# Places of their own for the values' matmuls in a gated attention and convolution block

## The chip, the core and the metric

The kernel runs on one core of one Trainium2 chip. The time is device time in microseconds (us), the median of several runs. Times inside the program come from one profiled execution.

The engines are named as the profile does: PE is TensorE (PEld its weight loads), DVE is VectorE, ACT is ScalarE, POOL is GpSimd and SP is SyncE, which here only issues DMAs.

## The reference

One layer on 2048 tokens of width 1024, float32. A normalised input is projected into nine parts. Two branches use them: a gated causal convolution of width 3, and attention of 16 query heads on 4 key heads of size 64, each query seeing the last 128 positions and a learned sink. Each branch is multiplied by a SiLU gate, projected, and the two are merged by sigmoid gates, projected once more and added to the input.

```python
h = rms_norm(x, norm_g)
u = jnp.einsum('bsd,dc->bsc', h, w_in)
v_c, b_c, c_c, z_c, q, k, v, z_a, gate_logits = jnp.split(u, SPLIT_POINTS, axis=-1)
y_c = b_c * causal_depthwise_conv(c_c * v_c, conv_w) * jax.nn.silu(z_c)
y_a = jnp.einsum('bsc,cd->bsd', y_c, w_conv_out)
# q and k: rms_norm per head; 128-position blocks, each with the block before it
scores = jnp.einsum('bnqhgd,bnkhd->bnhgqk', qb, kb) * scale
scores = jnp.where(valid[None, :, None, None], scores, NEG_INF)
m = jnp.maximum(jnp.max(scores, axis=-1, keepdims=True), sink)
p = jnp.exp(scores - m)
p = p / (jnp.sum(p, axis=-1, keepdims=True) + jnp.exp(sink - m))
out = jnp.einsum('bnhgqk,bnkhd->bnqhgd', p, vb)
y_b = jnp.einsum('bsc,cd->bsd', o, w_attn_out)       # o: out times its SiLU gate
merged = g_a * y_a + g_b * y_b
return x + jnp.einsum('bsd,de->bse', merged, w_out)
```

## The kernel before

The tokens are worked in two tiles of 1024 (`t` = 0 and 1), each in two halves of 512. A projection of 256 columns is a unit of seven products (a fast scheme of seven in place of eight). [...] The first projection of the first tile has eight plain products; a few units near the start and the end run in pairs.

The order of the work is written out by hand. A counter, `tick`, goes up by one with each product (`run`, L699). Everything else is put on a list under a count (`put`, L693) and is issued right behind the product with that count: in the order in which it was put, three functions first, then the second half of a weight's preparation, then the rest. A "place" in what follows is such a count, relative to the start of the tile. Each engine takes its instructions strictly in this order.

Attention is 32 steps in each tile: four key heads, eight blocks of 128 queries, in that order (`r` = 8 j + b). `attention` (L1657) puts the parts of a step relative to the place `n` of its scores, which stands in `AT0` and `AT1` (L96 to L101):

- n - 5, `att_load`: SP loads queries and keys (L1006 to L1023); n + 4, `att_load_v`: SP loads the values
- n, `att_scores`: six matmuls into the one score tile of PSUM (`ps_s`, one buffer), then on DVE the mask, the maximum and small sums
- n + 1, `att_exp`: four exponentials on ACT (L1079), which read the score tile
- n + 2, `att_norm` and `att_flip`: DVE scales the probabilities and turns 32x32 blocks, and POOL stores them to DRAM (L1099); n + 4, `att_back`: POOL gathers them back turned (L1106)
- n + 9, `att_turn`: ACT casts (L1113, L1114); n + 10, `att_low`: the low part on DVE and four selects on POOL that mask what lies outside the window (L1127)
- n + 13, `att_values`: six matmuls of 256 columns into a bank of `ps_m` (three buffers), L1144
- n + 14, `att_out`: two copies out of PSUM on ACT (L1153); n + 15, `att_sum`: SP stores one half to DRAM, and two places later POOL adds the other half to it (L1160)

The offsets are constants: `V_, F_, B_, X_, L_, O_, S_ = 4, 2, 4, 9, 10, 13, 15` (L57). The step's tiles, among them the four operands of its values, come from a pool of 19 slots in SBUF (`big`), which all results and loads share. A step's functions are put before those of the next step, so where values and a later step's scores have the same place, the values come first.

Of the kernel before, what the change touches and what calls it, by code (L numbers as in the profile page):

```python
# [56 lines left out]
V_, F_, B_, X_, L_, O_, S_ = 4, 2, 4, 9, 10, 13, 15  # L57
# [35 lines left out]
K_WAIT = 10  # L93
H_UP = 3
SUM_WAIT = 6
AT0 = [  # L96
    51, 56, 62, 66, 72, 78, 82, 87, 93, 99, 103, 108, 113, 119, 123, 127, 130, 135, 139, 142, 146, 149,
    153, 156, 160, 164, 167, 170, 174, 177, 181, 184]
AT1 = [
    41, 48, 56, 61, 67, 72, 75, 81, 84, 87, 90, 96, 99, 105, 109, 115, 119, 123, 126, 129, 132, 138,  # L100
    141, 144, 147, 150, 154, 157, 161, 164, 168, 174]  # L101
EVAC = {(0, 0): 3, (1, 1): 4, (0, 1): 5, (1, 0): 6}


# [1 line left out]
def block_kernel(  # L106
# [31 lines left out]
    def slot(shape, dt, name):  # L138
        return big.tile(shape, dt, tag="big", name=name)
# [7 lines left out]
    def mbank(name):  # L147
        return ps_m.tile([P, HB, P], F32, tag="m", name=name)
# [24 lines left out]
    def hs(q):  # L173
        return slice(q * H, (q + 1) * H)
# [178 lines left out]
    def wpair(name):  # L353
        return [wpool.tile([P, KP * UC], F32R, tag="w", name=f"{name}{i}") for i in "hl"]
# [338 lines left out]
    def put(n, f):  # L693
        at.setdefault(max(n, tick[0] + 1), []).append(f)
# [306 lines left out]
    def att_load(t, j, b):  # L1001
        nm = f"{t}_{j}_{b}"
        gb = t * NB + b
        kz = lows[(j * NB + b) % 2]
        q2 = slot([P, 2, 2, P], F32R, f"q2_{nm}")
        nc.sync.dma_start(  # L1006
            q2.bitcast(F32).rearrange("p h c x -> p (h c x)"),
            q2d[t][j][:, 2 * b : 2 * b + 2].rearrange("p h c e x -> p (h c e x)"))

        kq = slot([P, 2, 2 * P], F32R, f"kq_{nm}")  # L1010
        for c in range(2):
            nc.sync.dma_start(
                kq[HALVES[c], 1].bitcast(F32).rearrange("p (h x) -> p h x", h=2),
                q2d[t][j][LH, 2 * b : 2 * b + 2, c].rearrange("p h e x -> p h (e x)"))

        blocks = [(t, b - 1, 0, 2)] if b else [(t, 0, 1, 1)]
        if b == 0 and gb > 0:
            blocks.append((t - 1, NB - 1, 0, 1))
        for kt, k0, to, n in blocks:
            here, there = slice(to * P, (to + n) * P), slice(k0 * P, (k0 + n) * P)  # L1020
            nc.sync.dma_start(kq[:, 0, here].bitcast(F32), kd[kt][j, :, 0, there])
            for c in range(2):
                nc.sync.dma_start(kz[HALVES[c], c, here].bitcast(F32), kd[kt][j, HALVES[c], 1, there])  # L1023
        return q2, kq, kz
# [113 lines left out]
    def att_values(t, j, b, pcv, v2):  # L1138
        xh, xl, y = pcv
        po = mbank(f"po{t}_{j}_{b}").rearrange("p g q -> p (g q)")  # L1140
        for h in range(2):
            cs = slice(h * 2 * P, (h + 1) * 2 * P)
            for n, (kind, xx) in enumerate(((2 + h, xh), (h, y), (2 + h, xl))):
                nc.tensor.matmul(  # L1144
                    po[:, cs], lhsT=v2[:, kind, :], rhs=xx[:, :, h * HD : (h + 1) * HD],
                    start=h == 0 and n == 0, stop=n == 2, skip_group_check=h == 1)
        return po

    def att_out(t, j, b, po):
        pov = po.rearrange("p (h e s c q) -> p h e s c q", h=2, e=2, s=2, c=2)  # L1150
        o = slot([P, 2, 2, P], F32, f"o{t}_{j}_{b}")
        for e in range(2):
            nc.scalar.copy(o[:, :, e].rearrange("p c (h s q) -> p h s c q", h=2, s=2), pov[:, :, e])  # L1153
        return o

    def att_sum(t, j, b, o):
        to = od[t][2 * j : 2 * j + 2, :, b * P : (b + 1) * P].rearrange(
            "c (e d) q -> d (c e) q", d=HD)
        nc.sync.dma_start(to, o[LH].rearrange("p c e q -> p (c e) q"))
        put(tick[0] + ADD_WAIT, lambda: nc.gpsimd.dma_start(  # L1160
            to, o[UH].rearrange("p c e q -> p (c e) q"), accum_op=ALU.add))
# [307 lines left out]
    for t in range(NT):  # L1469
# [9 lines left out]
        for word in (SEQ0, SEQ1)[t].split():  # L1479
            both_ = word.split("+")  # L1480
            for name in both_:
                if len(both_) > 1:
                    paired.add(len(plan))
                key, j = name.rstrip("0123456789"), int(name[-1]) if name[-1].isdigit() else None
                if key in ("ya", "yb"):
                    w = w_co if key == "ya" else w_ao
# [9 lines left out]
    for n in range(S // P // 2):  # L1496
        t, c0 = divmod(2 * n * P, T)
# [7 lines left out]
    def x_state(t):  # L1505
        return state.setdefault(t, {"raw": {}, "ops": {}, "x": {}, "ss": {}})
# [31 lines left out]
    for n in range(KC // 2):  # L1538
        u, h = divmod(n, 2)
        if n < KP - KV_BIG:  # L1540
            live[0] += 2
            w = [[v[:, p * H : (p + 1) * H] for p in range(2)] for v in wpair(f"wkv{n}")]
        else:
            w = [[slot([P, H], F32R, f"wkv{n}_{p}{i}") for p in range(2)] for i in "hl"]
# [109 lines left out]
        ((0, 0), (0, 1), (1, 0), (1, 1), (0, 2), (0, 3), (1, 2), (1, 3)),  # L1654
        ((0, 0), (1, 0), (0, 1), (1, 1), (0, 2), (1, 2), (0, 3), (1, 3)))[KV_ORDER]], kv.banks))

    def attention(t, places):  # L1657
        for r, n in enumerate(places):
            j, b = divmod(r, NB)
            got = {}  # L1660

            def step(k, f, got=got):
                def g():
                    got[k] = f(got)
                return g

            put(n - 5, step("l", lambda g, j=j, b=b: att_load(t, j, b)))
            put(n + V_, step("v", lambda g, j=j, b=b: att_load_v(t, j, b)))
            put(n, step("s", lambda g, j=j, b=b: att_scores(t, j, b, g["l"])))
            put(n + 1, step("e", lambda g, j=j, b=b: att_exp(t, j, b, g["s"])))  # L1670
            put(n + 2, step("n", lambda g: att_norm(g["e"])))
            put(n + F_, step("f", lambda g, j=j, b=b: att_flip(t, j, b, g["n"])))
            put(n + B_, step("b", lambda g, j=j, b=b: att_back(t, j, b, g["f"])))
            put(n + X_, step("x", lambda g, j=j, b=b: att_turn(t, j, b, g["b"])))
            put(n + L_, step("w", lambda g: att_low(g["x"])))
            put(n + O_, step("o", lambda g, j=j, b=b: att_values(t, j, b, g["w"], g["v"])))
            put(n + O_ + 1, step("z", lambda g, j=j, b=b: att_out(t, j, b, g["o"])))
            put(n + S_, step("t", lambda g, j=j, b=b: att_sum(t, j, b, g["z"])))

    def paired_units(units):  # L1680
        (ka, oa, fa), (kb, ob, fb) = units
# [3 lines left out]
    for t in range(NT):  # L1685
        ops = state[t]["ops"]
        ys, opa, opb = {}, {}, {}
        t0 = tick[0] + 1 if t else 1
        a0 = t0 + (14 if t else 0)
        attention(t, [a0 + n for n in (AT0, AT1)[t]])  # L1690

        def unit_of(name, at_of):
            key, j = name.rstrip("0123456789"), int(name[-1]) if name[-1].isdigit() else None
            o = {"ya": opa, "yb": opb}.get(key, ops)
            if key == "k":
                return (key, t), o, fin_k(t)
            if key == "v":
                return (key, t), o, fin_v(t)
            if key == "q":
                fin = fin_q(t, j)  # L1700
            elif key == "cv":
                fin = fin_cv(t, j, ys)
            elif key == "b":
                fin = fin_b(t, j, ys)
            elif key in ("ga", "gb"):
                fin = fin_g(t, int(key == "gb"), j)
            elif key == "z":
                fin = fin_z(t, j, lambda k, q: yd[t][k, :, hs(q)], "z", ("c", t), ycd[t], at_of, nc.sync)
            elif key == "za":
                fin = fin_z(t, j, lambda k, q: od[t][k, :, hs(q)], "za", ("a", t), ocd[t], at_of, nc.gpsimd)  # L1710
            else:
                fin = fin_y(t, int(key == "yb"), j, at_of)
            return (key, t, j), o, fin

        if t + 1 < NT:
            h_stats(t + 1, tick[0] + STATS_AT)
        for word in (SEQ0, SEQ1)[t].split():
            n = tick[0] + 1
            if word == "z0":
                (h_prep if t + 1 < NT else w_prep)(*((t + 1,) if t + 1 < NT else ()), tick[0])  # L1720
            if word == "za2+za3":
                load_set(("c", t), n, opa)
            if word == "ya2+ya3":
                load_set(("a", t), n, opb)
            if word == "yb2+yb3":
                load_set(("h", t + 1) if t + 1 < NT else ("w", 0), n, x_state(t + 1)["ops"])
            names = word.split("+")
            if len(names) > 1:
                paired_units([
                    unit_of(name, lambda e, i=i, n=n: n + 2 * e + i) for i, name in enumerate(names)])  # L1730
            elif t == 0 and word == "q0":
                run(qunit(("q", 0, 0), ops, fin_q(0, 0)))
            else:
                run(sunit(*unit_of(word, lambda e, n=n: n + e)))
# [58 lines left out]
```

## Time and profile before

| | us |
|---|---|
| median of 3 runs | 1880.72 |
| range of the runs | 1880.46 to 1881.01 |
| the profiled execution | 1880.86 |
| its span, first to last instruction | 1878.9 |
| PE busy | 1872.3 |
| DVE busy | 1539.0 |
| ACT busy | 990.7 |
| POOL busy | 728.6 |

Matmuls are pipelined, so the durations of neighbours overlap: how long a group of them holds PE is read from the starts of what comes before and after it, not from a sum of durations. In rows in order of time the first column is the start in us from the span's start, the second the duration in us, and after the operation come the tiles (output<-inputs), the shapes and the count of instructions merged into the row. A bracket at the end is idle time of the engine just before, and what ended it. A row "A <- B: x, n, y" among the waits says that A waited x us for B in n cases, the longest y.

### The profile page before, as it was taken

How to read it: one execution, taken by the hardware profiler on the slowest of the kernel's cores; microseconds unless marked ns; L12 is line 12 of the kernel's file. 1: busy time of each engine (PE TensorE's matmuls, PEld its weight loads, DVE VectorE, ACT ScalarE, POOL GpSimd, SP SyncE). 2: the span in 40 equal slices, each digit the busy share in tenths (PEclk: the TensorE clock that was granted, in tenths of full speed). 3: DMA queues.
4: the chain of work that ended last, by engine and by line, in shares of the span. 5: the costliest groups of instructions: out<-in, count | busy, mean ns of one | idle time of the engine just before them, and what ended most of it. 6: DMA issues, size and time to landing. Idle time of an engine off the chain costs nothing.

```text
span 1878.9 us, 27817 instructions
## 1 busy us (share of the span) xinstructions
PE 1872.3 (100%) x8590; PEld 1560.2 (83%) x8590; DVE 1539.0 (82%) x2540; ACT 990.7 (53%) x2005; POOL 728.6 (39%) x1034
## 2 busy tenths in 40 slices
PE   9999999999999999999999999999999999999999
PEld 7888888888888888888888888888888888888887
DVE  7999888888887889878589988888887779887654
ACT  7665555556765354445456646556566346344321
POOL 2373454457667111021075535655676211121000
PEclk9999999999999999999999999999999999999999
DMA  8785566689989978899367557758888869989653
GB/s 312 181 230 176 146 177 199 179 251 274 275 247 269 319 270 296 281 290 296 101 191 230 179 167 216 206 159 246 254 238 245 279 246 346 320 263 284 221 174 110
DMA packets 270596, 438.96 MB, mean 234 GB/s; under 512 B 42032, under 2 KB 133168, under 8 KB 270448
## 3 DMA queue, kind: packets, MB, share of 16 engines
q1 hardware_dynamic: 211296, 316.23, 51.1%
q0 software_dynamic: 59008, 120.91, 24.8%
q8 instruction: 69, 1.13, 0.2%
q14 instruction: 79, 0.65, 0.1%
q10 hardware_dynamic: 144, 0.03, 0.0%
HBM read 279.48 MB, written 154.42 MB: 231 GB/s over the span
## 4 chain that ended last, share of the span: by engine, by line
PE 96%; DVE 2%; DMA 1%; issue 1%; ACT 0%; SPq 0%; POOL 0%; DVEq 0%; ACTq 0%; POOLq 0%
PE Y L483 33%; PE Vcv L483 5%; PE Xcv L483 5%; PE s L1055 3%; PE po L1144 2%; PE Xgb L483 2%; PE Vgb L483 2%; PE Xz L483 2%; PE Xb L483 2%; PE Vb L483 2%; PE Vga L483 2%; PE Xga L483 2%; PE Vz L483 2%; PE Vo L483 2%; PE Xo L483 2%; PE Xyb L483 2%
## 5 line engine op out<-in xcount | busy, mean ns | idle before, releaser
L1106 POOL DMA_DIRECT2D x<-fd x256 | 143.7, 607 | 80.3 <-DMA fd<-f 37.3
L1127 POOL TENSOR_SCALAR_AFFINE_SELECT xh<-xh 64x512 fp32r<-64x512 f32 x64 | 66.8, 1044 | 127.8 <-DVE xl L265 98.1
L1079 ACT ACTIVATE p<-s,st,rq 128x128 f32<-128x128 f32 x256 | 112.9, 451 | 1.9 <-DMA lows<-kd 1.9
L1099 POOL DMA_DIRECT2D fd<-f x64 | 38.4, 600 | 166.1 <-DVE f L265 158.4
L483 PE MATMUL Xcv<-oph,wcv_ah 128*128 128x512 f32 x256 | 79.0, 390 | 0.0
L1160 POOL DMA_DIRECT2D od<-o x64 | 69.6, 1094 | 19.1 <-ACT zs L1310 7.8
L883 POOL DMA_DIRECT2D q2d<-q_h x56 | 38.8, 692 | 73.8 <-ACT q_h L875 63.1
L1350 POOL DMA_DIRECT2D md<-thyb x32 | 27.4, 873 | 100.7 <-DVE thyb L265 79.0
L1127 POOL TENSOR_SCALAR_AFFINE_SELECT xl<-xl 64x512 fp32r<-64x512 f32 x64 | 63.0, 984 | 4.4
L1127 POOL TENSOR_SCALAR_AFFINE_SELECT yp<-yp 64x512 fp32r<-64x512 f32 x64 | 57.7, 901 | 4.2
L1127 POOL TENSOR_SCALAR_AFFINE_SELECT yp<-xl 64x512 fp32r<-64x512 f32 x64 | 55.8, 872 | 3.1
L483 PEld LDWEIGHTS Xcv<-oph,wcv_ah 128*128 128x128 f32 x256 | 47.6, 188 | 9.5
L265 DVE SCALAR_TENSOR_TENSOR y<-u,cols,y 128x512 f32<-128x512 f32 x64 | 51.5, 805 | 3.7 <-ACT y L1189 2.5
L265 DVE TENSOR_TENSOR opa<-ina,opa 128x512 fp32r<-128x512 f32 x56 | 36.2, 687 | 20.9 <-ACT opa L300 20.9
L265 DVE TENSOR_TENSOR p<-p,st 128x512 f32<-128x512 f32 x64 | 49.3, 770 | 2.7
L1079 ACT ACTIVATION_READ_ACCUMULATOR p<-s,st,rq 128x1 f32 x256 | 51.1, 200 | 0.0
L365 ACT CAST wcv_sh<-wcv_raw 128x1024 fp32r<-128x1024 f32 x16 | 16.9, 1054 | 63.0 <-DVE wcv_raw L265 63.0
L483 PE MATMUL Xcv<-oph,wcv_al 128*128 128x512 f32 x128 | 49.9, 390 | 0.0
L265 DVE STREAM_TRANSPOSE f<-p 128x512 f32<-128x512 f32 x64 | 45.5, 710 | 2.6 <-DVE p L265 0.2
L265 DVE TENSOR_TENSOR opc<-inc,opc 128x512 fp32r<-128x512 f32 x56 | 36.2, 687 | 13.8 <-ACT opc L300 10.3
L483 PE MATMUL Y<-oph,wcv_d 128*128 128x512 f32 x192 | 46.5, 391 | 0.0
L265 DVE TENSOR_REDUCE st<-s 128x4 f32<-128x512 f32 x64 | 44.2, 691 | 2.0
(792 smaller groups left out, 6590.9 us busy)
## 6 DMA issues: line engine op xcount, KB each, us to landing
wcv_raw<-in_w_in SPq DMA_DIRECT2D x32, 512.0 KB, 4.4
q<-q2d SPq DMA_DIRECT2D x64, 256.0 KB, 4.5
v<-vd SPq DMA_DIRECT2D x128, 128.0 KB, 4.3
fd<-f POOLq DMA_DIRECT2D x64, 256.0 KB, 3.9
x<-fd POOLq DMA_DIRECT2D x256, 64.0 KB, 3.3
gd<-th SPq DMA_DIRECT2D x64, 256.0 KB, 3.3
wq_raw<-in_w_in SPq DMA_DIRECT2D x16, 512.0 KB, 5.3
kq<-q2d SPq DMA_DIRECT2D x128, 64.0 KB, 4.4
```

Source lines behind the costliest of these rows:

```text
L265: r = f(*args, **kw)
L365: return (lambda: nc.scalar.copy(hi, src), lambda: vec.tensor_tensor(out=lo, in0=src, in1=hi.bitcast(F32), op=ALU.subtract))
L483: nc.tensor.matmul(ps, lhsT=w[:, j, :], rhs=b[:, m, :], start=start and j == 0 and i == 0, stop=j == KP - 1 and i == 2, skip_group_check=n ...
L883: (nc.sync if t == j == 0 else nc.gpsimd).dma_start(q2d[t][j][half, q * 2 * HB : (q + 1) * 2 * HB, i, e, :], src[HALVES[e]].bitcast(F32).r ...
L1055: nc.tensor.matmul(to, lhsT=w, rhs=x_, start=n == 0, stop=n == 2, skip_group_check=h == 1)
L1079: nc.scalar.activation(out=p[:, i, :], in_=sg[:, i, HD : 3 * HD], func=AF.Exp, bias=st[:, 1, i : i + 1], scale=rv[:, i // 2, i % 2 : i % 2 ...
L1099: nc.gpsimd.dma_start(fd, f)
L1106: nc.gpsimd.dma_start(x[QUADS[k]], src[k])
L1127: nc.gpsimd.affine_select(out=d4, in_=s4, pattern=[[0, 2], [-32 * sg, 2], [0, G], [-sg, 32]], compare_op=ALU.is_gt if prev else ALU.is_ge, ...
L1144: nc.tensor.matmul(po[:, cs], lhsT=v2[:, kind, :], rhs=xx[:, :, h * HD : (h + 1) * HD], start=h == 0 and n == 0, stop=n == 2, skip_group_c ...
L1160: put(tick[0] + ADD_WAIT, lambda: nc.gpsimd.dma_start(to, o[UH].rearrange("p c e q -> p (c e) q"), accum_op=ALU.add))
L1350: nc.gpsimd.dma_start(md[t][k, :, hs(q)], m, accum_op=ALU.add)
```

## The change

The values' matmuls no longer come at a fixed distance behind the scores. Each step has a place of its own for them, in `AV0` and `AV1`; the copies out of PSUM, the store and the accumulating store keep their distances from the values (1, 2 and 4 places). The places of the scores change as well, by up to three, and with them everything that is put relative to them.

```diff
-AT0 = [
-    51, 56, 62, 66, 72, 78, 82, 87, 93, 99, 103, 108, 113, 119, 123, 127, 130, 135, 139, 142, 146, 149,
-    153, 156, 160, 164, 167, 170, 174, 177, 181, 184]
-AT1 = [
-    41, 48, 56, 61, 67, 72, 75, 81, 84, 87, 90, 96, 99, 105, 109, 115, 119, 123, 126, 129, 132, 138,
-    141, 144, 147, 150, 154, 157, 161, 164, 168, 174]
+AT0 = [51, 56, 62, 66, 72, 78, 82, 87, 91, 96, 104, 109, 113, 119, 122, 126, 130, 134, 138, 141, 146, 149, 153, 156, 159, 164, 167, 170, 173, 177, 181, 183]
+AT1 = [41, 48, 56, 61, 67, 72, 75, 81, 85, 88, 91, 97, 100, 106, 110, 116, 120, 124, 126, 129, 133, 138, 141, 144, 147, 150, 154, 157, 160, 163, 167, 173]
+AV0 = [66, 72, 75, 82, 87, 91, 96, 100, 104, 109, 119, 122, 126, 132, 138, 141, 143, 149, 153, 156, 159, 164, 167, 170, 173, 177, 181, 183, 186, 190, 194, 197]
+AV1 = [56, 61, 72, 75, 81, 85, 88, 97, 100, 101, 104, 110, 116, 120, 124, 129, 133, 138, 139, 144, 147, 151, 154, 157, 160, 163, 167, 170, 173, 176, 180, 186]
...
-    def attention(t, places):
-        for r, n in enumerate(places):
+    def attention(t, places, values):
+        for r, (n, o) in enumerate(zip(places, values)):
             j, b = divmod(r, NB)
...
-            put(n + O_, step("o", lambda g, j=j, b=b: att_values(t, j, b, g["w"], g["v"])))
-            put(n + O_ + 1, step("z", lambda g, j=j, b=b: att_out(t, j, b, g["o"])))
-            put(n + S_, step("t", lambda g, j=j, b=b: att_sum(t, j, b, g["z"])))
+            put(o, step("o", lambda g, j=j, b=b: att_values(t, j, b, g["w"], g["v"])))
+            put(o + 1, step("z", lambda g, j=j, b=b: att_out(t, j, b, g["o"])))
+            put(o + S_ - O_, step("t", lambda g, j=j, b=b: att_sum(t, j, b, g["z"])))
...
-        attention(t, [a0 + n for n in (AT0, AT1)[t]])
+        attention(t, *([a0 + n for n in at_] for at_ in ((AT0, AV0), (AT1, AV1))[t]))
```

## The prediction

> **What bounds the kernel now.** I read the page's busy times, clock and chain first, then TensorE's waits, then its instructions in order of time around the attention's matmuls.
>
> ```profile
> span 1878.9 us, 27817 instructions
> PE 1872.3 (100%) x8590; PEld 1560.2 (83%) x8590; DVE 1539.0 (82%) x2540; ACT 990.7 (53%) x2005; POOL 728.6 (39%) x1034
> PEclk9999999999999999999999999999999999999999
> PE 96%; DVE 2%; DMA 1%; issue 1%; ACT 0%; SPq 0%; POOL 0%; DVEq 0%; ACTq 0%; POOLq 0%
> ```
>
> TensorE is busy throughout, at full clock in every slice, and 96% of the chain that ended last is its own.
>
> ```profile
> PE Y L1525 <- DVE zero L182: 1.5, 1, 1.5
> PE Vq L483 <- DVE wq_sl L265: 0.5, 1, 0.5
> ...
> PE Y L483 <- DVE yap L265: 0.2, 1, 0.2
> ```
>
> These are the first, second and last rows of what TensorE waited for: no score and no value matmul stands there. So the program lasts as long as the row of matmuls does, and a change counts in two ways: it alters how long that row takes with nothing to wait for, or it puts a wait into it. The number of matmuls, their shapes and their work stay as they are.
>
> The unit of time is one product of twelve matmuls, which is one place in the lists that the change edits:
>
> ```profile
> 602.88 0.61 PE L483 MATMUL Xz<-oph,wz_ah 128*128 128x512 f32 x2
> ...
> 605.60 0.61 PE L483 MATMUL Vz<-oph,wz_sh 128*128 128x512 f32 x2
> ...
> 608.32 0.61 PE L483 MATMUL Y<-oph,wz_sh 128*128 128x512 f32 x2
> ```
>
> Starts of undisturbed products lie 2.72 us apart.
>
> **What a neighbour is worth.** The six score matmuls (L1055) of a step and its six value matmuls (L1144) are put between products. I price a group from its own start to the start of the second product behind it, less one undisturbed product. That takes in whatever the group does to the product that follows it.
>
> ```profile
> 232.06 0.33 PE L1055 MATMUL s<-lows,kq 128*128 128x384 f32 x1
> ...
> 232.85 2.92 PE L483 MATMUL Y<-oph,wb_d 128*128 128x512 f32 x12
> 235.62 0.28 PE L1144 MATMUL po<-xh,v 128*128 128x256 f32 x1
> ...
> 236.33 0.63 PE L483 MATMUL Xcv<-oph,wcv_ah 128*128 128x512 f32 x2
> ...
> 239.08 0.61 PE L483 MATMUL Vcv<-oph,wcv_sh 128*128 128x512 f32 x2
> ...
> 1082.77 0.28 PE L1144 MATMUL po<-xh,v 128*128 128x256 f32 x1
> ...
> 1083.49 0.34 PE L1055 MATMUL s<-lows,kq 128*128 128x384 f32 x1
> ...
> 1084.28 2.91 PE L483 MATMUL Y<-oph,wcv_d 128*128 128x512 f32 x12
> 1087.03 0.61 PE L483 MATMUL Xb<-oph,wb_ah 128*128 128x512 f32 x2
> ...
> 1433.25 0.28 PE L1144 MATMUL po<-xh,v 128*128 128x256 f32 x1
> ...
> 1437.50 0.62 PE L483 MATMUL Vz<-oph,wz_sh 128*128 128x512 f32 x2
> ```
>
> Scores alone: 235.62 - 232.06 - 2.72 = 0.84 us. Values alone: 239.08 - 235.62 - 2.72 = 0.74 us. Values directly in front of scores, which the kernel before has seven times: 1087.03 - 1082.77 - 2.72 = 1.54 us, and in the last of them 1437.50 - 1433.25 - 2.72 = 1.53 us. Worked in nanoseconds from the same rows, every merged group costs 1533, every one of 37 undisturbed groups of values 739 or 740, and 40 of 44 of scores 833 (the other four are the narrow first blocks, at 700). So a merge saves 833 + 740 - 1533 = 40 ns. Where it comes from can be seen: inside the merged group nothing is saved, but the product behind scores takes 235.62 - 232.85 = 2.77 us and the one behind a merged group 1087.03 - 1084.28 = 2.75 us, so two slowed products become one.
>
> [...]
>
> **The change, part by part.** The lists in the diff, with the old rule that values come 13 places behind their scores, give the count of merges: 1 of 32 steps in the first tile and 6 in the second before, 24 and 24 after (values whose place stands in the scores' list of the tile). That is 48 - 7 = 41 more, so 41 x 0.040 = 1.64 us less. Both ends for the two merges with narrow scores, which no row shows: 0 and 0.07 us each, the slow-down behind both groups being some 0.04 and 0.03; I take 0.04.
>
> Scores move by at most three places, values by up to four, and with them every instruction that hangs on them: a step's loads on SP's queue, its exponentials and casts on ACT, its mask and four gathers on POOL, its store and accumulating store. Their number doesn't change. ACT (53%) and POOL (39%) have room in total; what matters is what arrives late somewhere, and there are three such things.
>
> First, scores. All scores share one PSUM tile, so a step's scores wait until the previous step's exponentials have read theirs. Before, neighbours were at least three places apart. After, two pairs are two apart: 181 and 183 in the first tile, 124 and 126 in the second. From the end of a score group (0.36 us after its last matmul's start) to the start of the next lies 2 x 2.72 + 0.83 - 0.96 = 5.31 us in the second tile, where 0.96 is 1084.09 + 0.36 - 1083.49 by the rows here and above. In the first tile values stand in front of the second scores, which gives 5.31 + 0.74 = 6.05 us. How long the exponentials take:
>
> ```profile
> 1084.09 0.36 PE L1055 MATMUL s<-lows,kq 128*128 128x384 f32 x1
> 1320.27 0.36 PE L1055 MATMUL s<-lows,kq 128*128 128x384 f32 x1
> 1100.63 0.33 PE L1055 MATMUL s<-lows,kq 128*128 128x384 f32 x1
> ...
> 1101.22 0.36 PE L1055 MATMUL s<-lows,kq 128*128 128x384 f32 x1
> 550.97 0.36 PE L1055 MATMUL s<-lows,kq 128*128 128x384 f32 x1
> 1200.11 0.36 PE L1055 MATMUL s<-lows,kq 128*128 128x384 f32 x1
> ```
>
> ```profile
> 1089.66 0.46 ACT L1079 ACTIVATE p<-s,st,rq 128x128 f32<-128x128 f32 x1
> 1325.83 0.45 ACT L1079 ACTIVATE p<-s,st,rq 128x128 f32<-128x128 f32 x1
> 1109.32 0.45 ACT L1079 ACTIVATE p<-s,st,rq 128x128 f32<-128x128 f32 x1
> 551.79 0.65 ACT L1153 COPY o<-po 128x256 f32<-128x256 f32 x2
> 554.87 0.21 ACT L1076 ACTIVATE st<-st 128x4 f32<-128x4 f32 x1 [2.42 <-DVE st L265]
> 556.28 0.46 ACT L1079 ACTIVATE p<-s,st,rq 128x128 f32<-128x128 f32 x1
> 558.48 0.62 ACT L1113 CAST xh<-x 128x512 fp32r<-128x512 f32 x1
> 1203.85 0.45 ACT L1079 ACTIVATE p<-s,st,rq 128x128 f32<-128x128 f32 x1
> ```
>
> The end of the last exponential less the end of the scores is 8.19 us at its longest (1109.77 - 1101.58) and 3.83 at its shortest (1204.30 - 1200.47). It goes with the place inside a projection's seven products, since ACT and DVE prepare weights there: place 124 is the sixth of seven, and the four scores that stood sixth in the second tile before took 4.85 to 5.96 us, the first 5.67 (1090.12 - 1084.45), the last 5.66, their mean 5.54. So scores at 126 would wait 5.54 - 5.31 = 0.23 us, with the ends at 0 and 8.19 - 5.31 = 2.88. For the first tile the step at 181 stays where it is, with 5.41 us (556.74 - 551.33) against 6.05: no wait. The copies of the output (0.65 us) already stand ahead of its exponentials, and the casts of another step (0.62 us and as much again) that now come ahead too fit into the 2.42 us that ACT waits there for DVE. Without that cover 5.41 + 1.24 - 6.05 = 0.60 us. Behind a waiting score stand the next product and all that follows.
>
> Second, values wait for POOL's masks. The tightest cases before:
>
> ```profile
> 501.30 0.76 POOL L1127 TENSOR_SCALAR_AFFINE_SELECT xl<-xl 64x512 fp32r<-64x512 f32 x1
> 1153.31 0.76 POOL L1127 TENSOR_SCALAR_AFFINE_SELECT xl<-xl 64x512 fp32r<-64x512 f32 x1
> ```
>
> ```profile
> 502.58 0.28 PE L1144 MATMUL po<-xh,v 128*128 128x256 f32 x1
> 1155.97 0.28 PE L1144 MATMUL po<-xh,v 128*128 128x256 f32 x1
> ```
>
> The masks end 0.52 us ahead at the first, which the change gives a place more. Of the 64 steps 29 get one to three places more and 35 keep 13; the tightest of those 35 has 1155.97 - 1154.07 = 1.90 us. POOL would have to be that much later there before TensorE notices. I take 0.
>
> Third, holding. A step's four operands of the values live up to three places longer, and their SBUF slots are free later for loads and results. No wait of TensorE goes back to that now. I take 0, with one product (2.72 us) as the other end.
>
> Sum: -1.64 + 0.23 = -1.41 us. The profiled execution took 1880.86 us (span 1878.9 and 1.96 around it), 0.14 over the median of 1880.72; so 1879.45 for it and **1879.3 us** as a median, 0.07% less. A measurement of this kernel tells about 0.2% (3.76 us) from no change, so this counts as the same.
>
> **The rivals.** (a) The merges are given back by one wait: scores two places apart. It decides at the second tile's pair, once the exponentials end later than 5.31 + 1.64 = 6.95 us after the scores; from there on the kernel is slower than before. For it: the output's copies stand ahead of most exponentials now, and the longest row is 8.19. Against it: the sixth place of that tile was never over 5.96. At 8.19 the time is 1880.72 - 1.64 + 2.88 = 1882.0.
>
> (b) A merge saves nothing, because the slowed product belongs to any dense stretch and doubles with its length. Against it: seven merged groups at 1533 ns. Time: 1880.72 + 0.23 = 1881.0. [...]
>
> (c) Masks come late. Two score pairs closer together crowd POOL. If it were 3 us later everywhere, the margins of the 35 unmoved values would be short by 5.7 us in all: 1879.3 + 5.7 = 1885.0. Against it: for any wait at all it takes 1.9 us.
>
> (d) Loads or products wait for held slots, one product's length: 1879.3 + 2.7 = 1882.0.
>
> (e) The matmuls don't come to stand together, because something of TensorE's lies between values and scores in one place. The only others are turnings: of keys and values early in a tile, of the norms after the first tile's last scores. Time: 1880.7 plus 0.2.
>
> **How the numbers follow.** The forecast 0.64 (from 1878.9, with no wait, to 1880.2), (a) 0.13, (b) 0.06, (c) 0.08, (d) 0.06, (e) 0.03. The likeliest is 1879.3. The low end, 1878.6, is the full 1.64 with the narrow merges at their upper end and the 0.3 us by which single runs lie below the median; the high end, 1882.2, takes in (a), (b), (d) and (e) and leaves out most of (c) and the worst of (a). Faster by over 0.2% would need 3.76 us, and no row offers more than 41 x 0.07 = 2.9: 0.04. Slower by over 0.2% is (c) in most of its size and two bad waits of (a) or (d): 0.09. Within: 0.87.
>
> **What would show it.** Right: 48 merged groups at 1533 ns, 16 alone of each kind, no score or value among TensorE's waits except scores near the 126th place of the second tile with some tenths; a span of about 1877.5. Wrong: a wait of over 1.6 us there (a); merged groups at 1573 ns (b); values waiting for masks in POOL's rows (c); products waiting for weights prepared late on ACT or DVE, which I priced at nothing.

## The result, and the profile after

| us | before | after |
|---|---|---|
| median | 1880.87 (4 runs, 1880.46 to 1881.40) | 1906.21 (4 runs, 1904.59 to 1909.31) |
| the profiled execution | 1880.86 | 1909.31 |
| its span | 1878.9 | 1906.8 |
| groups of values directly in front of scores | 7 | 48 |
| idle stretches of PE over 0.1 us, in all | 3.0 | 20.1 |
| half clock granted | none | 13.65 |

The ratio is 1.0135 (95% interval 1.0124 to 1.0147): the kernel became 25.3 us slower, where 1.4 us less was forecast. Lines above the lists have their old numbers in the changed kernel, those behind stand two earlier (PE's products are L481, scores L1053, values L1142).

The page of the kernel after: its span, the busy times and the chain that ended last.

```profile
span 1906.8 us, 27817 instructions
PE 1883.0 (99%) x8590; PEld 1564.2 (82%) x8590; DVE 1538.6 (81%) x2540; ACT 989.6 (52%) x2005; POOL 735.6 (39%) x1034
PE 85%; DVE 5%; DMA 4%; issue 2%; ACT 2%; POOL 1%; SPq 0%; ACTq 0%; DVEq 0%; POOLq 0%
```

The counts of instructions are the same and so is the work of DVE and ACT. PE's own share of the chain fell from 96% to 85%; DVE, DMA and ACT have taken it. What PE waited for, kernel after:

```profile
PE Y L481 <- DVE b L263: 4.2, 1, 4.2
PE Y L481 <- ACT Y L504: 3.2, 2, 2.2
PE po L1142 <- POOL yp L1125: 2.5, 2, 2.2
PE s L1053 <- ACT p L1077: 2.3, 1, 2.3
PE po L1142 <- POOL xl L1125: 1.7, 2, 1.3
```

Before, the longest was the 1.5 us at the start. Now four single waits are over 2 us (the row of ACT's Y holds one of them, of 2.2), and only one of them is a score's. The span grew by 27.9 us: 17.1 is idle time of PE, 6.8 is an estimate for the 13.65 us at half clock (half of it is lost, as the product of 4.60 us below shows), and 1.6 goes off for the merges; that leaves 5.6 us, which lies in PE's busy time and which I haven't assigned.

Whether the change did what it says is seen in PE in order of time, a merged group of the kernel after:

```profile
259.27 0.28 PE L1142 MATMUL po<-xh,v 128*128 128x256 f32 x1
259.99 0.34 PE L1053 MATMUL s<-lows,kq 128*128 128x384 f32 x1
...
263.53 0.62 PE L481 MATMUL Y<-oph,wcv_sh 128*128 128x512 f32 x2
```

It costs 263.53 - 259.27 - 2.72 = 1.54 us, as the seven groups of before did.

**The half clock.** PE in order of time, kernel after, and the same time in slices of a microsecond (busy time and count of each engine, granted clock, DMA share, GB/s):

```profile
1339.23 0.36 PE L1053 MATMUL s<-lows,kq 128*128 128x384 f32 x1
1343.78 4.60 PE L481 MATMUL Y<-oph,wb_d 128*128 128x512 f32 x12 [4.19 <-DVE b L263]
```

```profile
1344.00:1345.00 1.00, 1.00 (x4) 0.77 (x4) 1.00 (x2) 0.00 (x0) 1.00 (x3) 0.59 0.55 166
1345.00:1346.00 1.00, 1.00 (x4) 0.80 (x3) 0.93 (x3) 0.00 (x0) 1.00 (x2) 0.50 0.75 177
...
1347.00:1348.00 1.00, 1.00 (x5) 0.78 (x4) 1.00 (x3) 1.00 (x2) 0.00 (x0) 0.70 0.84 200
```

The product behind the wait takes 4.60 us, where one behind scores took 2.92 in the prediction's rows. Its slices have a clock of 0.50 for 2 x (0.41 + 0.30) + 2 = 3.42 us, and 4.60 - 2.92 = 1.68 us come on top of the wait. In this profile each of the four waits over 2 us (2.22, 2.17, 2.30 and 4.19) has such a stretch behind it, and no shorter wait has one; other runs below don't keep to that, as the last section shows. The page's row of the clock is the same before and after, since its slices are 48 us long.

**Where the waits come from.** Three are followed back here, each in the kernel after; the fourth, which ends at 414 us, stands at the place that the experiments on order look at. First, values that wait for their masks (DVE, POOL and PE in order of time):

```profile
483.25 0.72 DVE L263 STREAM_TRANSPOSE f<-p 128x512 f32<-128x512 f32 x1 [5.89 <-DMA od<-o]
...
484.27 0.60 POOL L1097 DMA_DIRECT2D fd<-f  x1 [5.14 <-DVE f L263]
487.06 1.69 POOL L1125 TENSOR_SCALAR_AFFINE_SELECT yp<-xl 64x512 fp32r<-64x512 f32 x1
...
488.80 0.38 PE L1142 MATMUL po<-yp,v 128*128 128x256 f32 x1 [2.17 <-POOL yp L1125]
```

`f` is written by DVE from `p`; it has nothing to do with the store of an output `o`, except that it gets a slot of `big`. The release by that store says that the slot was `o`'s and that its accumulating store was not done. DVE stands 5.89 us with all that is queued behind it, POOL, which has the masks behind `f`'s store, stands 5.14 us, and in the end the values wait.

Second, the wait of 4.19 us above: DVE's `b` got the slot of a result `y` whose store was under way. DVE:

```profile
1337.71 0.71 DVE L263 STREAM_TRANSPOSE f<-p 128x512 f32<-128x512 f32 x1 [4.02 <-issue]
...
1343.03 0.69 DVE L263 TENSOR_TENSOR b<-Y,s5b 128x512 f32<-128x512 f32 x1 [2.83 <-DMA yd<-y]
```

`b` reads the PSUM tile Y, and the next product writes it. The slot accounts for 2.83 of the 4.19 us; without it `b` would still have been some 1.4 us late, behind a DVE that had stood 4.02 us just before, for a reason that the profile doesn't name.

Third, the scores at 183 in the first tile (PE, then ACT and DVE in order of time):

```profile
562.53 0.36 PE L1053 MATMUL s<-lows,kq 128*128 128x384 f32 x1
571.36 0.45 PE L1053 MATMUL s<-lows,kq 128*128 128x384 f32 x1 [2.30 <-ACT p L1077]
...
565.73 0.69 ACT L1217 ACTIVATE th<-Xga,hbias 128x512 f32<-128x512 f32 x1 [4.30 <-PE Y L481]
566.32 0.61 ACT L363 CAST wz_d<-wz_raw 128x512 fp32r<-128x512 f32 x1
...
566.96 0.69 DVE L263 TENSOR_TENSOR wz_d<-wz_raw,wz_d 128x512 fp32r<-128x512 f32 x1 [4.06 <-ACT wz_d L363]
569.34 0.21 ACT L1074 ACTIVATE st<-st 128x4 f32<-128x4 f32 x1 [0.70 <-DVE st L263]
...
570.76 0.46 ACT L1077 ACTIVATE p<-s,st,rq 128x128 f32<-128x128 f32 x1
```

The exponentials of the step at 181 end 8.33 us behind its scores (571.22 - 562.89), not 5.41 as before. Their sums on DVE stand behind a weight's `wz_d`, and that behind the same weight's cast on ACT, which stands behind the tanh of a result. In the kernel before the tanh began 0.3 us after its product had given way to the next group of matmuls (550.70 and 550.38); here it begins 4.5 us after that (565.73 and 561.22), released by the next product. Whether it waited for a slot there, the trace doesn't say.

**Stores that hold slots.** A view that the prediction didn't use is the idle time of DVE and ACT that ends with a store of `o`, `y` or `f`. The instructions released read none of these stores' data; they write tiles that get slots of `big`, so by the inferred releaser this is time lost to slots. The kernel before, all five rows:

```profile
DVE b L265 <- DMA fd<-f: 2.0, 1, 2.0
ACT th L1219 <- DMA fd<-f: 2.6, 1, 2.6
ACT xh L1113 <- DMA od<-o: 2.5, 1, 2.5
ACT yp L1114 <- DMA od<-o: 2.3, 2, 1.8
ACT o L1153 <- DMA od<-o: 0.6, 1, 0.6
```

The kernel after, its four largest:

```profile
DVE f L263 <- DMA od<-o: 5.9, 1, 5.9
DVE b L263 <- DMA yd<-y: 2.8, 1, 2.8
...
ACT p L1077 <- DMA od<-o: 5.8, 3, 3.4
ACT p L1077 <- DMA fd<-f: 4.7, 1, 4.7
```

The sum is 10.0 us before and 26.4 after; I call it "slot waits" below. The count isn't complete: idle time of ACT and DVE in front of tiles of `big` for which the profile names no releaser ("issue") is left out, 23.9 us before and 26.8 after. Before, no slot wait was over 2.6 us, and apart from the 1.5 us at the start TensorE waited 0.5 us at most for anything. The pool had little slack already.

### The profile page after: what moved, and what is told of

Its sections match the earlier page's. It is cut to its first block, busy times and chain, and to the rows that moved or that the text cites. A ratio compares the mean times of both kernels' runs of the same rounds, so it can differ in the third digit from the quotient of the medians.

```text
span 1906.8 us, 27817 instructions
## 1 busy us (share of the span) xinstructions
PE 1883.0 (99%) x8590; PEld 1564.2 (82%) x8590; DVE 1538.6 (81%) x2540; ACT 989.6 (52%) x2005; POOL 735.6 (39%) x1034
## 4 chain that ended last, share of the span: by engine, by line
PE 85%; DVE 5%; DMA 4%; issue 2%; ACT 2%; POOL 1%; SPq 0%; ACTq 0%; DVEq 0%; POOLq 0%
PE Y L481 29%; PE Vcv L481 4%; PE Xcv L481 4%; PE s L1053 2%; PE Xz L481 2%; PE Vz L481 2%; PE Xza L481 2%; PE Vo L481 2%; PE Xo L481 2%; PE Vza L481 2%; PE Xga L481 2%; PE po L1142 2%; PE Xb L481 2%; PE kv L570 2%; PE Xgb L481 2%
## 5 line engine op out<-in xcount | busy, mean ns | idle before, releaser
L1097 POOL DMA_DIRECT2D fd<-f x64 | 42.9, 671 | 137.4 <-DVE f L263 134.2
L481 PE MATMUL Xcv<-oph,wcv_ah 128*128 128x512 f32 x256 | 78.9, 390 | 0.0
L1125 POOL TENSOR_SCALAR_AFFINE_SELECT yp<-xl 64x512 fp32r<-64x512 f32 x64 | 62.0, 968 | 3.1
L481 PEld LDWEIGHTS Xcv<-oph,wcv_ah 128*128 128x128 f32 x256 | 47.9, 188 | 9.5
L263 DVE TENSOR_TENSOR xl<-x,xh 128x512 fp32r<-128x512 f32 x64 | 43.6, 681 | 7.7 <-ACT wga_th L363 2.2
L481 PE MATMUL Xcv<-oph,wcv_al 128*128 128x512 f32 x128 | 49.8, 389 | 0.0
L1053 PE MATMUL s<-lows,kq 128*128 128x384 f32 (+2 forms) x128 | 44.3, 346 | 2.7 <-ACT p L1077 2.3
```

What stands on the lines that cost most here:

```text
L263: r = f(*args, **kw)
L481: nc.tensor.matmul(ps, lhsT=w[:, j, :], rhs=b[:, m, :], start=start and j == 0 and i == 0, stop=j == KP - 1 and i == 2, skip_group_check=n ...
L1053: nc.tensor.matmul(to, lhsT=w, rhs=x_, start=n == 0, stop=n == 2, skip_group_check=h == 1)
L1097: nc.gpsimd.dma_start(fd, f)
L1125: nc.gpsimd.affine_select(out=d4, in_=s4, pattern=[[0, 2], [-32 * sg, 2], [0, G], [-sg, 32]], compare_op=ALU.is_gt if prev else ALU.is_ge, ...
```

## The experiments

In the expectations, H is the theory that slots of `big` are held too long, P that the scores' new places do the harm by themselves, and C that the output's copies in front of the exponentials do. The order of the work on ACT, DVE and POOL in general is what is left if all three fall short; the later expectations call it Q. Medians in us; the kernel before ran again beside each group of kernels, at 1880.7 to 1881.1. "Over" is the difference from it; slot waits, merged groups, PE's idle time and the time at half clock (without a stretch that begins in the last 2 us of the span) are of the profiled execution. Single runs of one changed kernel lie up to 6.7 us apart (place_135, 1892.9 to 1899.6), so a few us between two of them decide nothing.

| kernel | median | ratio (95%) | over | slot waits | merged | PE idle | half clock |
|---|---|---|---|---|---|---|---|
| after | 1906.21 | 1.0135 (1.0124 to 1.0147) | 25.3 | 26.4 | 48 | 20.1 | 13.65 |
| scores_only | 1895.05 | 1.0078 (1.0055 to 1.0101) | 13.9 | 15.6 | 20 | 11.2 | 3.4 |
| values_only | 1896.64 | 1.0081 (1.0052 to 1.0111) | 15.5 | 25.8 | 53 | 14.4 | 3.4 |
| hold_15 | 1907.17 | 1.0137 (1.0108 to 1.0167) | 26.1 | 53.4 | 17 | 20.1 | 17.1 |
| copies_behind | 1904.83 | 1.0125 (1.0095 to 1.0155) | 23.7 | 26.6 | 48 | 19.2 | 10.2 |
| after_20 | 1895.08 | 1.0077 (1.0047 to 1.0106) | 14.4 | 24.8 | 48 | 12.8 | 6.8 |
| hold_20 | 1890.82 | 1.0052 (1.0029 to 1.0075) | 10.1 | 13.7 | 17 | 11.1 | 0 |
| before_20 | 1884.26 | 1.0020 (1.0009 to 1.0032) | 3.5 | 7.6 | 7 | 5.4 | 0 |
| before_18 | 1902.55 | 1.0116 (1.0087 to 1.0146) | 21.8 | 41.5 | 7 | 17.0 | 6.8 |
| late_casts | 1912.42 | 1.0168 (1.0138 to 1.0197) | 31.4 | 28.1 | 48 | 23.0 | 10.2 |
| values_late | 1910.34 | 1.0157 (1.0127 to 1.0186) | 29.3 | 31.1 | 53 | 23.7 | 17.1 |
| values_14 | 1890.59 | 1.0053 (1.0034 to 1.0073) | 9.6 | 24.1 | 26 | 9.2 | 0 |
| scores_20 | 1884.76 | 1.0022 (1.0010 to 1.0035) | 3.7 | 5.8 | 20 | 6.8 | 3.4 |
| after_v8 | 1900.35 | 1.0099 (1.0071 to 1.0128) | 19.6 | 20.2 | 48 | 14.7 | 0 |
| hold_v8 | 1890.72 | 1.0046 (1.0023 to 1.0069) | 9.9 | 16.4 | 17 | 10.2 | 0 |
| before_v8 | 1883.36 | 1.0015 (1.0003 to 1.0026) | 2.6 | 4.6 | 7 | 5.8 | 3.4 |
| after_20_v8 | 1897.38 | 1.0087 (1.0061 to 1.0113) | 16.6 | 5.8 | 48 | 14.9 | 6.8 |
| place_135 | 1896.13 | 1.0077 (1.0043 to 1.0110) | 15.1 | 26.5 | 48 | 14.9 | 10.2 |
| values_20 | 1899.82 | 1.0095 (1.0072 to 1.0118) | 18.8 | 20.7 | 53 | 17.2 | 6.8 |

### The parts of the change alone

scores_only has the new places of the scores, and values 13 behind them as in the kernel before (here and below some lists are written as the rule that gives them):

```diff
+AV0 = [n + 13 for n in AT0]
+AV1 = [n + 13 for n in AT1]
```

> The places of the scores are those of the change, and the values come 13 places behind their scores again, as in the kernel before: 20 merges in place of 48 (7 before), no step is held longer. Theory P (the new places of the scores are to blame: scores stand where ACT and DVE are busy with weights, and two pairs are only two places apart): most of the loss stays, 15 to 25 us over before. Theory H (operands held longer, so that slots of the pool come free late): within 3 us of before. Theory C (the output's copies in front of the exponentials on ACT): a third of the loss, 4 to 8 us over before.

values_only keeps the scores' old places and moves values alone, 13 to 16 behind, so that 53 groups are merged:

```diff
+AV0 = [66, 72, 78, 82, 87, 93, 95, 103, 108, 113, 119, 123, 127, 135, 139, 142, 146, 149, 153, 156,
+       160, 164, 167, 170, 174, 177, 181, 184, 187, 190, 194, 197]
+AV1 = [56, 61, 72, 75, 81, 87, 90, 96, 99, 100, 105, 109, 115, 119, 123, 129, 132, 138, 141, 144,
+       147, 154, 157, 158, 161, 164, 168, 170, 174, 177, 181, 187]
```

> The scores keep the places of the kernel before; the values go to the first place of a later step's scores that is 13 to 16 places behind their own scores: 53 merges, and 90 step-places of longer holding in sum against 52 in the change. Theory P: the merges bring what they promised, 46 x 0.04 = 1.8 us under before, to 1879. Theory H: worse than the change, 25 to 40 us over before. Theory C: 20 to 30 us over before, as there are as many merges as in the change.

hold_15 keeps the scores' places too and has all values 15 behind, so that what is late is not what is merged:

```diff
+AV0 = [n + 15 for n in AT0]
+AV1 = [n + 15 for n in AT1]
```

> The scores keep the places of the kernel before; every step's values come 15 places behind them in place of 13: 17 merges in place of 7, and 128 step-places of longer holding in sum against 52 in the change. Theory P: 10 x 0.04 = 0.4 us under before. Theory H: 30 us or more over before. Theory C: 3 to 6 us over before.

copies_behind is the change with the two copies out of PSUM put behind the exponentials of the same place:

```diff
-            put(o + 1, step("z", lambda g, j=j, b=b: att_out(t, j, b, g["o"])))
+            copies.append((o + 1, step("z", lambda g, j=j, b=b: att_out(t, j, b, g["o"]))))
...
+        for n, f in copies:
+            put(n, f)
```

> The change as it is, but the copies of the values out of PSUM are issued behind all other attention functions of their place, so behind the exponentials that they stood in front of on ACT. Theory C: the loss goes, within 4 us of before. Theories P and H: the loss stays, 20 to 30 us over before.

Measured: 13.9 and 15.5 us over for the two halves of the change, each a loss by itself; no theory had a range that holds either. hold_15, with 17 merged groups and every score where it was, loses as much as the whole change (26.1, where H had 30 or more), so merging is not what costs. Order of time on ACT and then PE, hold_15:

```profile
594.71 0.62 ACT L1112 CAST yp<-x 64x512 fp32r<-64x512 f32 x1 [6.21 <-DMA od<-o]
597.30 0.59 ACT L504 COPY Y<-Xz 128x512 f32<-128x512 f32 x1
...
597.94 0.80 PE L481 MATMUL Y<-oph,wz_sh 128*128 128x512 f32 x2 [3.18 <-ACT Y L504]
```

A cast gets a slot of an `o` that is still being stored, ACT stands 6.21 us, and the copy into Y, queued behind, lets PE wait 3.18 us. copies_behind gives 1.6 us back, with intervals that overlap: theory C falls as the main cause.

### One slot more, one fewer

For a twentieth slot one of the two spare tiles that hold a sum (`s5`) is given up, and a unit that runs beside another takes a slot in its place. The same is done to the unchanged kernel, which shows the price of the edit itself.

```diff
-    big = ctx.enter_context(tc.tile_pool(name="big", bufs=19))
+    big = ctx.enter_context(tc.tile_pool(name="big", bufs=20))
...
-    def spare(name):
-        return consts.tile([P, H], F32, tag="s5", bufs=2, name=name)
+    def spare(name, other=False):
+        if other:
+            return slot([P, H], F32, name)
+        return consts.tile([P, H], F32, tag="s5", bufs=1, name=name)
...
-        s5 = spare(f"s5{nm}")
+        s5 = spare(f"s5{nm}", other)
```

> The change with 20 slots in the shared pool in place of 19 (the room comes from the second buffer of the spare tile of a projection, which only paired units need; there it takes a slot). Theory H (the pool runs out: an instruction gets the slot of a result whose store is not done, and its engine's whole queue waits): half of the loss or more goes, under 1893. Theory P (places of the scores): the loss stays, 1900 to 1910.

> The kernel with scores as before and values 15 places behind, with 20 slots. Theory H: from 1907 to under 1890, and the waits of ACT for the accumulating store go. Theory P has no word on it, since the scores are where they were; a third theory Q (the later values fall among other work in the queues, whatever the slots) says that it stays within 5 us of 1907.

> Control: the kernel before with 20 slots. Theory H: 0 to 4 us faster than before, as it hardly waits for a slot; P and Q: the same, within 2 us.

before_18 changes the unchanged kernel in one number:

```diff
-    big = ctx.enter_context(tc.tile_pool(name="big", bufs=19))
+    big = ctx.enter_context(tc.tile_pool(name="big", bufs=18))
```

> The kernel before with 18 slots in place of 19, nothing else changed. Theory H: slower by 10 us or more, with waits of ACT and DVE for stores. Theories P and Q: within 3 us of before.

Measured: one slot fewer costs the kernel before 21.8 us, with every place as it was. Among its waits, of DVE, ACT and PE:

```profile
DVE f L265 <- DMA od<-o: 3.7, 1, 3.7
ACT th L1219 <- DMA fd<-f: 6.3, 1, 6.3
...
PE Y L483 <- DVE yap L265: 7.8, 2, 5.2
```

So a pool that is one slot short makes such waits by itself. One slot more takes 16.0 us from hold_15 (26.1 to 10.1, 6.6 above before_20) and 10.9 from the change. So holding is a cause. It isn't all: after_20 stays 10.9 us above before_20, and after_20 and hold_20 (1895.1 and 1890.8) stay just above H's bounds of 1893 and 1890. H also had before_20 at 0 to 4 us faster; it is 3.5 slower, so the edit has a price of its own.

### Holding less in other ways

late_casts is the change, and values_late is values_only, with the loads of the values, the casts and the masks put relative to the values and not to the scores, so that operands are held no longer than before (the gathered probabilities, one tile, are held longer in their place):

```diff
-            put(n + V_, step("v", lambda g, j=j, b=b: att_load_v(t, j, b)))
+            put(o - O_ + V_, step("v", lambda g, j=j, b=b: att_load_v(t, j, b)))
...
-            put(n + X_, step("x", lambda g, j=j, b=b: att_turn(t, j, b, g["b"])))
-            put(n + L_, step("w", lambda g: att_low(g["x"])))
+            put(o - O_ + X_, step("x", lambda g, j=j, b=b: att_turn(t, j, b, g["b"])))
+            put(o - O_ + L_, step("w", lambda g: att_low(g["x"])))
```

> The change with 19 slots, but a step's load of values, its casts and its masks keep their distances to its values (9, 4 and 3 places ahead) in place of those to its scores. A step that waits longer then holds one tile longer (the gathered probabilities), where the change holds four (the values and three operands). Theory H (slots): a good part of the loss goes, from 1906 to 1885 to 1896. Theory P (places of the scores): what the scores' places cost by themselves, 14 us, stays, 1893 to 1897. Theory Q (work falls elsewhere in the queues): 1900 or more.

> Scores where they were before, values merged as in the run that moved values only (53 merges), and load, casts and masks move with the values, so that one tile is held longer in place of four; 19 slots. Theory H: from 1896.6 to 1879 to 1887. Theory Q: 1893 or more.

values_14 keeps the scores' old places and moves values by one place at most, where that merges:

```diff
+AV0 = [n + 14 if n + 14 in AT0 else n + 13 for n in AT0]
+AV1 = [n + 14 if n + 14 in AT1 else n + 13 for n in AT1]
```

> Scores where they were before; values go to a later step's scores only where these are 13 or 14 places behind their own: 26 merges (7 before), 19 step-places of longer holding in sum against 90 in the run that moved values only; 19 slots. Theory H: a fifth of that run's 15.5 us, so 2 to 5 us over before, less 0.8 for the merges. Theory Q: 1888 or more.

scores_20 is scores_only with the slot more:

```diff
-    big = ctx.enter_context(tc.tile_pool(name="big", bufs=19))
+    big = ctx.enter_context(tc.tile_pool(name="big", bufs=20))
...
+        s5 = spare(f"s5{nm}", other)
```

> Only the scores moved, values 13 places behind them, 20 slots. Theory H: from 1895 to 1884 to 1888, as far as 20 slots take it in the kernel before (1884). Theory P: it stays at 1893 to 1897.

Measured: the two with late casts are the slowest of all (31.4 and 29.3). What PE waits for in late_casts:

```profile
PE po L1142 <- POOL yp L1125: 6.3, 4, 2.2
PE po L1142 <- POOL xl L1125: 5.3, 6, 1.5
```

Ten waits of values for masks, 11.6 us: the casts, up to three places later now, come to stand with other work, and the masks stand three places ahead of their values, where the change had up to six. Slot waits didn't fall either (28.1 and 31.1). So these two don't measure the holding. values_14 loses 9.6 us with 26 merged groups, more than the 2 to 5 that H had: either a single place of holding is felt, or the order of the work is. scores_20 stands 0.2 us above before_20, as H had it, so the scores' new places by themselves cost nothing that can be seen once there is a slot more: theory P falls.

### The loads of the values four places later

This shortens the holding of one operand and moves only an issue on SP's queue:

```diff
-V_, F_, B_, X_, L_, O_, S_ = 4, 2, 4, 9, 10, 13, 15
+V_, F_, B_, X_, L_, O_, S_ = 8, 2, 4, 9, 10, 13, 15
```

> The change with 19 slots, but each step loads its values 8 places behind its scores in place of 4, still 5 places (13.6 us) or more ahead of the values' matmuls. Only SP's queue changes; every step holds a slot 4 places shorter, 256 slot-places in sum, against 208 that the change holds more (52 places, four tiles). Theory H (slots run out): half of the loss or more goes, from 1906 to under 1893. Theory Q (the order of work in the queues of ACT, DVE and POOL, whatever the slots): within 4 us of 1906.

> Scores as before, values 15 places behind, loads of the values 8 behind, 19 slots. Theory H: from 1907 to under 1893; theory Q: within 4 us of 1907.

> Control: the kernel before with loads of the values 8 places behind the scores. Theory H: as with 20 slots, within 4 us of before on either side; Q: the same.

> The change with 20 slots and the values loaded 8 places behind the scores. Theory H: 1879 to 1887, so that nothing is left that slots do not explain. Theory Q: what 20 slots left, 10 us or more over before.

Measured: 16.2 us off hold_15, about what the slot gave (16.0), and 5.7 off the change, between H (under 1893) and Q (within 4 us of 1906). With both, the change's slot waits are down to 5.8 us, less than the 10.0 of the kernel before, and it still stands 16.6 us over. The longest slot wait of that run is 1.8 us, and idle time without a named releaser in front of tiles of `big` is 25.0 us there, against 23.9 before. PE's largest waits in after_20_v8 (the edit for the slot moves the lines behind it down by two):

```profile
PE Y L481 <- ACT Y L506: 4.2, 4, 2.6
PE Vcv L481 <- DVE y L263: 1.9, 1, 1.9
PE Y L481 <- DVE b L263: 1.7, 1, 1.7
```

H alone falls as the whole explanation. Nor do the repairs add: after_20 with 24.8 us of slot waits is no slower than after_20_v8 with 5.8.

### Order, at one place

In after_20 the largest wait of PE for ACT stands at 414 us. There the step whose scores are at 134 (135 before) has its exponentials in front of ACT's copy into Y. place_135 puts this one step back:

```diff
-AT0 = [51, 56, 62, 66, 72, 78, 82, 87, 91, 96, 104, 109, 113, 119, 122, 126, 130, 134, 138, 141, 146, 149, 153, 156, 159, 164, 167, 170, 173, 177, 181, 183]
+AT0 = [51, 56, 62, 66, 72, 78, 82, 87, 91, 96, 104, 109, 113, 119, 122, 126, 130, 135, 138, 141, 146, 149, 153, 156, 159, 164, 167, 170, 173, 177, 181, 183]
```

> The change with 20 slots and one number altered: the scores of step 17 of the first tile at place 135, where the kernel before had them, in place of 134. At 134 their exponentials are issued one product earlier, in front of ACT's copy into Y that the next projection's third product needs; in the profile with 20 slots that copy came at 413.6 us and TensorE lost 1.8 us there and more behind it. Theory Q (order): that wait goes, and 2 to 4 us with it, from 1895 to 1891 to 1893. Theory H (slots) has no word on a single place: the wait of TensorE at 412 us stays.

values_20 is values_only with the slot more (its diff is that of after_20):

> Scores where they were before, values merged as in the run that moved values only (53 merges, 1896.6 with 19 slots), with 20 slots. Theory H: 1881 to 1885, no more than the kernel before with 20 slots (1884.3) less the 1.8 us of the merges. Theory Q: over 1888.

ACT and PE in order of time, after_20, and then ACT in place_135:

```profile
413.20 0.46 ACT L1079 ACTIVATE p<-s,st,rq 128x128 f32<-128x128 f32 x1
413.64 0.60 ACT L506 COPY Y<-Xgb 128x512 f32<-128x512 f32 x1
...
414.29 0.73 PE L481 MATMUL Y<-oph,wgb_sh 128*128 128x512 f32 x2 [2.45 <-ACT Y L506]
```

```profile
410.68 0.58 ACT L506 COPY Y<-Xgb 128x512 f32<-128x512 f32 x1
411.39 0.44 ACT L1079 ACTIVATE p<-s,st,rq 128x128 f32<-128x128 f32 x1
```

The copy is some 3 us earlier and the wait is gone, so order at this place is shown as its cause. But the median is about the same, 1896.1 against 1895.1: other waits grew (one of DVE's `b` for a slot lets PE wait 4.3 us in that run, 3.7 in after_20). Q had 1891 to 1893 for it: two of the four runs lie at 1893 and two at 1899, the profiled one among the latter, so what the place is worth in time stays open. values_20 is not helped by the slot either: 18.8 us over, against 15.5 without it. Its largest wait, DVE and PE:

```profile
1303.50 0.71 DVE L263 STREAM_TRANSPOSE f<-p 128x512 f32<-128x512 f32 x1 [6.06 <-DMA od<-o]
...
1311.08 4.20 PE L481 MATMUL Y<-oph,wgb_d 128*128 128x512 f32 x9 [5.74 <-DVE th L263]
```

Still a slot: and over before_20 the loss is 15.3. One slot more doesn't make up for 49 of 64 steps whose operands are held one to three places longer. No version beats the kernel before.

## Why the prediction was wrong

- **The saving of a merge**: right. There are 48 merged groups, 40 of them at 1533 ns; of the 16 scores alone 13 cost 833, and of the 16 values alone 12 cost 739 or 740, as priced. So about 41 x 0.040 = 1.64 us is in the result. values_only shows that it can't be seen beside the rest: 53 merged and 15.5 us slower. Rivals (b) and (e) fall.
- **First, scores**: the second tile's pair loses 0.13 us, where I had 0.23. The first tile's pair waits 2.30, where I had none. The casts did fit into the cover that I named: behind them ACT still waits 0.70 us for DVE. What failed is that the 5.41 us of the old row were carried over to a place whose neighbours on ACT and DVE had moved. This is rival (a) in the other tile, and 2.3 of 25.3 us plus its half clock.
- **Second, masks**: waits of 4.2 us in all stand there, at values whose masks had been in time. The one that was followed back is 2.17 us of a DVE that stood for a slot 5.89 us earlier, not the crowding on POOL that rival (c) assumed.
- **"Third, holding"** is the step that failed: "I take 0, with one product (2.72 us) as the other end". The reason that I gave, that no wait of TensorE goes back to it, looked at one engine only. The runs show in its place a cost that is many times the other end: hold_15, which leaves the scores and moves all values two places, loses 26.1 us, and one slot more takes 16.0 of that away. The rows of DVE and ACT had 10.0 us of slot waits before the change, and before_18 shows how close to the edge that is. Rival (d) had the mechanism, and priced it as one event of one product. It is a wait of 3 to 6 us of an engine that takes its instructions in order, at several places, each passed on to masks, copies and weights.
- **What I priced at nothing without a step of its own**: ACT and DVE late for TensorE. As a sign of being wrong I named products that wait for weights; those waits grew only from 0.5 to 2.0 us. What I didn't name is larger, products that wait for DVE or ACT at the PSUM tile Y (through `b`, `th` and the copy into Y): 4.2, 0.9 and 3.2 us, 8.3 in all, and none of these before.
- **A term that the sum lacked**: the clock. Behind four waits over 2 us stand 13.65 us at half clock, 6.8 us by the estimate above.
- **The range** reached to 1882.2, as each of the rivals was taken as one event. The loss is more than three times what all five together would add (7.4 us). Its low end adds up to 1878.7 and not 1878.6, which changes nothing.

What stays open is how the 25.3 us divide. With slot waits below those of the kernel before, 16.6 us remain, and in those the two edits have a share of their own, 3.5 and 2.6 us where they were made singly. So by an estimate from these runs 9 to 15 us go with the slots and 10 to 17 with the order of the work, if the parts can be added at all, and after_20 beside after_20_v8 speaks against that. One sign of the order: DVE's sums wait for ACT's exponentials in 14 cases before, in 28 both in the kernel after and in after_20_v8, and in 20 in scores_20. That this is what costs is argued, not shown. A pool of more than 20 slots wasn't tried.

## What to carry to other kernels

Where TensorE is busy all the time, a gain of 0.04 us a place has to be weighed against the pools that the moved work draws on: read the waits of the engines off the critical path too, and look for those that end with a store of another tile: here they showed, before the change, a pool with little slack. A consumer that moves later holds its operands longer, and the price here was not the holding but the next instruction that was given a slot whose store wasn't done, with all that stood behind it on its engine: 5.89 us of DVE in the kernel after, 6.21 of ACT in hold_15. Take a slot away from the unchanged kernel first: here that cost 21.8 us, and holding the values' operands two places longer, in hold_15, 26.1.

## What was unexpected of the hardware

Behind waits of TensorE of no more than 2.17 to 2.30 us the granted clock was half, for 3.41 us each time. Slices of a microsecond behind the 2.17 us at 486 to 489 us and a further 0.44, kernel after:

```profile
490.00:491.00 1.00, 1.00 (x11) 1.00 (x10) 0.97 (x2) 0.95 (x3) 1.00 (x3) 0.93 0.90 329
491.00:492.00 1.00, 1.00 (x4) 0.81 (x4) 1.00 (x3) 1.00 (x2) 1.00 (x3) 0.50 0.99 203
...
494.00:495.00 1.00, 1.00 (x5) 0.79 (x4) 0.93 (x4) 0.00 (x0) 0.94 (x2) 0.87 1.14 233
```

That is 2 x (0.07 + 0.13) + 3 = 3.40 us at half clock. Read with finer edges, the four stretches of this profile begin at 415.77, 490.86, 572.78 and 1344.19 us, 0.41 to 1.42 us after the matmuls have begun again, and together last 13.65 us, 3.413 each. Their starts lie 75.09, 81.92 and 771.41 us apart: 22, 24 and 226 times that length, to within 0.1 us.

The length of a wait alone doesn't settle it, though. The wait of 2.45 us at 414 us in after_20 has full clock behind it:

```profile
415.00:416.00 1.00, 1.00 (x6) 0.80 (x5) 0.96 (x2) 0.70 (x1) 0.93 (x2) 1.00 1.02 336
```

The product behind the wait of 3.68 us in that run takes 5.49 us, 2.57 more than 2.92: so by an estimate some 5.1 of its 6.8 us at half clock, more than one stretch of 3.41, stand behind that wait. In scores_only, where no wait is over 1.9 us, 3.4 us are at half clock. Since the stretches of the kernel after lie on steps of 3.413 us, I take it that how a wait falls on such steps matters too; that is a guess of mine, and no run here tests it. By these runs a wait of about 2 us is priced at its length, or at that plus 1.7 us.
